# A decoder block on one Trainium2 core: residual rows parked in DRAM during the input projection, their SBUF lent to split weights

## The chip, the cores and the metric

The kernel runs on one core of a Trainium2 chip, as one program in one launch. The metric is the device time in microseconds (us) of an execution; lower is better. Three runs of the kernel before gave 1945.76, 1946.14 and 1946.44 us.

## The reference

One decoder layer over 256 rows (tokens) of 2048 features, in f32:

```python
h = h + 0.5 * swiglu(rms_norm(h, ffn1_norm), ffn1_w_gu, ffn1_w_down)     # D_FF = 5632
h = h + hybrid_mixer(rms_norm(h, mix_norm), w_in, ..., w_out)
h = h + 0.5 * swiglu(rms_norm(h, ffn2_norm), ffn2_w_gu, ffn2_w_down)
gate = sigmoid(rms_norm(h, ple_norm) @ ple_w_gate)
h = h + gate * (p @ ple_w_proj)
out = rms_norm(h, final_norm)
```

`hybrid_mixer` makes one input projection `n @ w_in` (14 blocks of 512 columns and 16 extra columns, a and b). Eight heads go through a short convolution, SiLU, normalisation and a gated delta rule in chunks of 64 rows, which needs a triangular system solved per chunk; eight heads go through stick-breaking attention. The two results, one of them gated, are concatenated and multiplied by `w_out` (4 blocks of 512 columns).

## The kernel before, in words

**Weights.** TensorE gets every f32 product as three matmuls of rounded operands: a weight W is split into `whi`, W rounded (a cast on ScalarE, ACT, line 74), and `wlo = W - whi` (a subtraction on VectorE, DVE, line 75). `weight_pair` (lines 64 to 76) handles a pair of 128-row slices, 128 x 1024 values or 512 KB: the load into a `raw` tile is issued on SP's queue (line 71), then come cast and subtraction. There are four `raw` buffers and three each of `whi` and `wlo`. `next_weights` (lines 82 to 97) hands out pairs in the order of the list `order` and emits loads and splits ahead of their use; with `LEAD = 2` the pair in use and two more are split. `accumulate` (lines 99 to 112) takes a pair and issues its 12 matmuls of 512 columns (lines 109 to 111: `whi` by the high part of the activations, `wlo` by the high part, `whi` by the low part).

**Stages.** The first feed-forward layer (`ffn`), the mixer (`mixer`, lines 746 to 1314), the second feed-forward layer, and the gated embedding with the final norm. The residual rows `h` lie in one SBUF tile of 128 x 2 x 2048 f32 (line 139). In the mixer `h` is read by the norm that precedes it (three of its four blocks by way of `transposed`, lines 162 to 186, the last on TensorE at line 212), and then not until the output projection adds to it (line 1310).

**The mixer's side work.** Each of the 14 column blocks of the input projection takes 8 pairs, 112 pairs in all. After each pair `lanes.step()` advances four lists of generators by one piece each: `conv_silu` (from line 927: transposes `tr_p` on TensorE, 12 multiply-adds on DVE at line 938, SiLU on ACT at line 944 or 947, transposes back `tr_b` at line 806), `decay_and_beta` (line 833: the 16 extra columns, whose weights `wabr` are loaded on ACT's queue at line 835, split into `wpad` at lines 852 and 853, and multiplied on TensorE at lines 848 and 849, `abT`), `system` and `chain` (the triangular solve, 31 steps of `pm` and `sol` on DVE at lines 1056 and 1058, then small matmuls), and `stick`. So TensorE's stream holds the pairs' matmuls with small matmuls of the side work between them, and these need results of DVE and ACT.

**Order.** The code is written in program order; a scheduler then fixes each engine's own order before the program is built. On the chip every engine, and every queue of transfers (SP's, ACT's, POOL's), runs its instructions in that order and waits at the first that isn't ready. `wo` are the products of the output projection; its third quarter of each block comes from `sbT` and the last from the second `dnT`, which `gate` (from line 1256) makes: multiply, transpose by way of DRAM (`scr`, then `yT`, on SP's queue), split (lines 1272 and 1273).

Of the kernel before, what the change touches and what calls it, by code (L numbers as in the profile page):

```python
# [34 lines left out]

NS_BEHIND = 2

PLAIN = {"1": 2, "2": 1}
EPS = 1e-6
QSCALE = P ** -0.5  # L40
# [3 lines left out]
def block_kernel(ctx, tc, a, out):  # L44
    nc = tc.nc
# [15 lines left out]
    dr = ctx.enter_context(tc.tile_pool(name="dr", bufs=1, space=bass.MemoryType.DRAM))  # L61


    def weight_pair(src, pool=wp, bufs=3, parts=1):

        raw = wp.tile([P, 2, NB], F32, tag="raw", name="raw", bufs=4)
        hi = pool.tile([P, 2, NB], F32R, tag="whi", name="whi", bufs=bufs)
        lo = pool.tile([P, 2, NB], F32R, tag="wlo", name="wlo", bufs=bufs)
        for i in range(parts):
            j = slice(2 * i // parts, 2 * (i + 1) // parts)  # L70
            nc.sync.dma_start(out=raw[:, j, :], in_=src[:, j, :])
        for i in range(parts):
# [9 lines left out]
    def next_weights():  # L82

        ahead = max(1, min(LEAD, done[1] // 2))
        while done[0] < len(order):
            kind, src = order[done[0]]
            if kind != "load" and sum(k == kind for k, _ in split) > (ahead if kind == "pair" else 1):
                break
            done[0] += 1
            if kind == "load":  # L90
                src()
            elif kind == "sum":
                split.append((kind, next(src.sums)))
            else:
                split.append((kind, weight_pair(src, parts=2 if not done[1] and not split else 1)))
        done[1] += 1
        return split.pop(0)[1]

# [37 lines left out]

    gains = cp.tile([P, 4, KD], F32, tag="gains", name="gains")
    nc.scalar.dma_start(out=gains, in_=a["gains"])
    h = act.tile([P, 2, D], F32, tag="h", name="h")

    ident = cp.tile([P, P], F32, tag="ident", name="ident")
    make_identity(nc, ident)
# [45 lines left out]
    def norm_block_behind(nT, which, j, tmp):  # L188

        hi, lo = nT  # L190
        yield
        tT = tmp()
        yield from transposed(lambda t: h[:, t, block(j)], tT)
        for kk in range(4):
            split_scaled(*(n[j][:, kk, :].rearrange("p (t q y) -> p (t q) y", t=2, q=4) for n in (hi, lo)),
                         tT[:, :, :, 32 * kk:32 * kk + 32].rearrange("p t q y -> p (t q) y"),
                         gains[:, which, 4 * j + kk:4 * j + kk + 1])
            if kk == 1:
                yield

    def norm_block(nT, which, j, tmp, new=mx_ps):

        if j < 3:
            lanes.add(0, norm_block_behind(nT, which, j, tmp))
            return
        hi, lo = nT
        for kk in range(2):
            tr = new("tr_n")
            for q in range(2):
                k = 4 * j + 2 * kk + q  # L210
                for t in range(2):
                    nc.tensor.transpose(tr[:, q * T + t * P:q * T + (t + 1) * P],
                                        h[:, t, k * P:(k + 1) * P], ident)
            for q in range(2):
                k = 4 * j + 2 * kk + q
                split_scaled(hi[j][:, 2 * kk + q, :], lo[j][:, 2 * kk + q, :],
                             tr[:, q * T:(q + 1) * T], gains[:, which, k:k + 1])

    def sumsq(stat, t, c, col):
        n = c.stop - c.start  # L220
        junk = act.tile([P, NB], F32, tag="junk", name="junk", bufs=1)
        nc.scalar.activation(junk[:, 0:n], h[:, t, c], AF.Square, accum_out=stat[:, t, col:col + 1])

    def block(j):
        return slice(j * NB, (j + 1) * NB)
# [185 lines left out]
        return made  # L411

    ffn_plan = {"1": plan("1")}
    order += [("pair", a["w_in"][blk][g]) for blk in W_IN_ORDER for g in range(KD // 2)]
    order += [("pair", a["w_out"][nb][g]) for nb in range(4) for g in range(KD // 2)]
    ffn_plan["2"] = plan("2")
    order += [("pair", a["w_pg"][2][g]) for g in range(KD // 2)] + [("pair", a["w_pp"][2])]
# [46 lines left out]
    def ffn(n, nT, r, scale, next_norm, stat):  # L464
        xs = picker(*nT)
        late = callable(r)
        with tc.tile_pool(name="ffn", bufs=1) as fp:
# [43 lines left out]
            for group, todo in ffn_plan[n]:  # L511
# [15 lines left out]
                for kind, one in todo:  # L527
# [19 lines left out]
                    if dn:  # L547
                        nb = group.nb + b
                        for t in range(2):
                            hb = h[:, t, block(nb)]  # L550
                            nc.vector.scalar_tensor_tensor(out=hb, in0=outs[t], scalar=scale, in1=hb,
                                                           op0=ALU.mult, op1=ALU.add)
                            if group.last:
                                sumsq(stat, t, block(nb), nb)
# [45 lines left out]
    def first_loads():  # L600

        todo = [(t, j) for t in range(2) for j in range(4)]
        xs_at = {2 * k - 1 if k < 4 else k + 3: 2 * k for k in range(1, KD // 2)}
        for i in range(1, 16):
            if i in xs_at:
                load_x(xs_at[i])
            if 5 <= i < 13:
                t, j = todo[i - 5]
                nc.sync.dma_start(out=h[:, t, block(j)], in_=a["x"][t * P:(t + 1) * P, block(j)])
            if 7 <= i < 15:  # L610
                t, j = todo[i - 7]
                sumsq(stat, t, block(j), j)
            yield
        r_first.append(rstd(stat))
# [4 lines left out]
    def r1():  # L619
# [8 lines left out]

    stat = new_stat()
    nT = mixer(tc, nc, a, act, mm_ps, mx_ps, accumulate, picker, new_nT, norm_block, sumsq, block, lanes, transposed,  # L630
               nT, r, h, stat, ident, mhalf)
    r = rstd(stat)

    stat = new_stat()
# [4 lines left out]
    with tc.tile_pool(name="fin", bufs=1) as fp:  # L639
# [18 lines left out]
        def gated(e, gt, c, t, col):  # L658

            n = c.stop - c.start  # L660
            s = act.tile([P, NB], F32, tag="nat", name="sg", bufs=4)[:, 0:n]
            nc.scalar.activation(s, gt, AF.Sigmoid, scale=r[:, t:t + 1])
            nc.vector.tensor_tensor(out=s, in0=e, in1=s, op=ALU.mult)
            nc.vector.tensor_tensor(out=h[:, t, c], in0=h[:, t, c], in1=s, op=ALU.add)
            sumsq(stat, t, c, col)
            nc.vector.tensor_tensor(out=hf[:, t, c], in0=h[:, t, c], in1=fg[:, c], op=ALU.mult)

        def embed(new):
            e = [new("e") for _ in range(2)]
# [74 lines left out]


def mixer(tc, nc, a, act, mm_ps, mx_ps, accumulate, picker, new_nT, norm_block, sumsq, block, lanes, transposed,
          nT, r, h, stat, ident, mhalf):
    xs = picker(*nT)
    C64 = P // 2
    CONV, CHAIN, STICK, SYSTEM = 0, 1, 2, 3  # L750
# [2 lines left out]
    with tc.tile_pool(name="mix", bufs=1) as mp, \  # L753
# [521 lines left out]
            dnT[1].append(tl)  # L1275


        lanes.add(CHAIN, decay_and_beta())
        for hg in range(2):
            for part in (1, 0, 2):  # L1280
# [12 lines left out]
            lanes.add(CONV, gate(y, hg))  # L1293


        nxt = new_nT()

        def pick(k):
# [6 lines left out]
        for nb in range(4):  # L1305
            d = [mm_ps("wo") for _ in range(2)]
            accumulate(d, pick, KD)
            for t in range(2):
                hb = h[:, t, nb * NB:(nb + 1) * NB]
# [68 lines left out]
```

## Time and profile before

| | |
|---|---|
| median of three runs | 1946.14 us (1945.76 to 1946.44) |
| span of the profiled execution, first to last instruction | 1944.1 us |
| median less span | 2.0 us |
| TensorE (PE) busy | 1927.9 us, 99% |
| DVE busy | 1603.2 us, 82% |
| ACT busy | 1163.4 us, 60% |
| moved by DMA | 475.06 MB, 244 GB/s on the mean |

The runs give no time for the profiled execution apart from its span; the median of the runs lies 2.0 us above the span, and these 2.0 us are taken as what lies around it. Busy time of PE is modelled from pipelined matmuls, each of which shows some 0.39 us though one starts about every 0.23 us; so what PE loses is read from the distance of starts. In a row of instructions the number in brackets is the idle time of the engine before it and what ended that. The input projection lies at about 694 to 1065 us of the span, the output projection at 1065 to 1154 us.

### The profile page before, as it was taken

The numbers are of one execution on the slowest core, as the hardware profiler recorded it, in microseconds if no ns is written. First come the engines' busy times: TensorE is split into PE (matmuls) and PEld (weight loads), VectorE is DVE, ScalarE is ACT, GpSimd is POOL, SyncE is SP. The second block draws the span as 40 slices with busy tenths as digits, with TensorE's granted clock in tenths as the row PEclk, the third lists the DMA queues.
The fourth block names the chain that finished last, engine by engine and source line by source line (L and its number), as shares of the span: only waits on it lengthen the run. The fifth ranks groups of instructions, "written<-read, shape, count | busy, mean of one in ns | idle before, by whom it ended". The sixth has DMA issues, their size and how long they took to land.

```text
span 1944.1 us, 24295 instructions
## 1 busy us (share of the span) xinstructions
PE 1927.9 (99%) x8882; PEld 1593.1 (82%) x8882; DVE 1603.2 (82%) x1743; ACT 1163.4 (60%) x1358; POOL 148.8 (8%) x226
## 2 busy tenths in 40 slices
PE   9999999999999999999999999999999999999998
PEld 7888888888888888878788888888888888888887
DVE  7879988998889866797856679899888998889965
ACT  6655656566665567654555456566565755657654
POOL 0010110000001000010100000011000100001000
PEclk9999999999999999999999999999999999999999
DMA  8778898898898765556464776788898988989864
GB/s 306 269 217 291 256 292 272 248 296 247 269 288 255 224 218 171 173 167 218 159 215 157 243 278 229 236 268 285 260 278 253 306 257 261 264 263 273 253 212 147
DMA packets 144183, 475.06 MB, mean 244 GB/s; under 512 B 19648, under 2 KB 47296, under 8 KB 129856
## 3 DMA queue, kind: packets, MB, share of 16 engines
q1 hardware_dynamic: 104896, 293.78, 43.6%
q0 software_dynamic: 25920, 160.44, 29.9%
q10 hardware_dynamic: 13248, 19.30, 3.3%
q8 instruction: 69, 1.13, 0.2%
q14 instruction: 50, 0.41, 0.1%
HBM read 451.44 MB, written 22.02 MB: 244 GB/s over the span
## 4 chain that ended last, share of the span: by engine, by line
PE 91%; DVE 6%; issue 1%; DMA 1%; ACT 1%; POOL 0%; SPq 0%; POOLq 0%; DVEq 0%; ACTq 0%
PE d L540 5%; PE d L541 5%; PE d L542 5%; PE u L541 5%; PE u L542 5%; PE u L540 5%; PE g L541 4%; PE g L542 4%; PE pj L109 4%; PE pj L110 4%; PE pj L111 4%; PE g L540 4%; PE g L335 4%; PE g L334 4%; PE g L336 4%; PE u L334 3%
## 5 line engine op out<-in xcount | busy, mean ns | idle before, releaser
L74 ACT CAST whi<-raw 128x1024 fp32r<-128x1024 f32 (+1 forms) x489 | 511.7, 1050 | 420.0 <-PE pj L111 108.9
L75 DVE TENSOR_TENSOR wlo<-raw,whi 128x1024 fp32r<-128x1024 f32 (+1 forms) x489 | 590.8, 1217 | 155.8 <-ACT whi L74 153.1
L296 DVE TENSOR_TENSOR slo<-R,shi 128x2048 fp32r<-128x2048 f32 (+2 forms) x224 | 444.4, 1987 | 99.9 <-ACT shi L295 99.7
L295 ACT CAST shi<-R 128x2048 fp32r<-128x2048 f32 (+2 forms) x224 | 374.0, 1673 | 185.6 <-DVE R L304 74.4
L109 PE MATMUL pj<-whi,nTh 128*128 128x512 f32 x448 | 179.4, 401 | 0.0
L110 PE MATMUL pj<-wlo,nTh 128*128 128x512 f32 x448 | 175.3, 391 | 1.4 <-DVE wlo L75 1.4
L111 PE MATMUL pj<-whi,nTl 128*128 128x512 f32 x448 | 174.9, 390 | 0.0
L541 PE MATMUL d<-wlo,hTh 128*128 128x512 f32 x448 | 174.4, 389 | 0.0
L542 PE MATMUL d<-whi,hTl 128*128 128x512 f32 x448 | 174.0, 389 | 0.0
L540 PE MATMUL d<-whi,hTh 128*128 128x512 f32 x448 | 173.1, 390 | 0.0
L541 PE MATMUL g<-wlo,nTh 128*128 128x512 f32 x400 | 156.1, 390 | 0.6 <-DVE wlo L75 0.6
L540 PE MATMUL g<-whi,nTh 128*128 128x512 f32 x400 | 154.9, 390 | 1.2 <-ACT whi L74 0.9
L542 PE MATMUL g<-whi,nTl 128*128 128x512 f32 x400 | 155.9, 390 | 0.0
L541 PE MATMUL u<-wlo,nTh 128*128 128x512 f32 x400 | 155.7, 389 | 0.1
L542 PE MATMUL u<-whi,nTl 128*128 128x512 f32 x400 | 155.6, 389 | 0.0
L540 PE MATMUL u<-whi,nTh 128*128 128x512 f32 x400 | 154.2, 389 | 0.0
L304 DVE TENSOR_TENSOR R<-R 128x2048 f32<-128x2048 f32 (+2 forms) x68 | 135.4, 1991 | 0.1
L110 PEld LDWEIGHTS pj<-wlo,nTh 128*128 128x128 f32 x448 | 84.2, 188 | 19.2 <-DVE wlo L75 3.0
L540 PEld LDWEIGHTS d<-whi,hTh 128*128 128x128 f32 x448 | 84.1, 188 | 17.9 <-ACT hTh L499 0.7
L542 PEld LDWEIGHTS d<-whi,hTl 128*128 128x128 f32 x448 | 84.1, 188 | 17.7
L111 PEld LDWEIGHTS pj<-whi,nTl 128*128 128x128 f32 x448 | 84.1, 188 | 17.5
L541 PEld LDWEIGHTS d<-wlo,hTh 128*128 128x128 f32 x448 | 84.1, 188 | 17.4
(327 smaller groups left out, 3482.5 us busy)
## 6 DMA issues: line engine op xcount, KB each, us to landing
raw<-in_w_gu SPq DMA_DIRECT2D x199, 512.0 KB, 5.7
raw<-in_w_down SPq DMA_DIRECT2D x112, 512.0 KB, 6.4
raw<-in_w_in SPq DMA_DIRECT2D x112, 512.0 KB, 3.4
R<-in_w_gu2q POOLq DMA_DIRECT2D x54, 1024.0 KB, 8.1
R<-in_w_gu1q POOLq DMA_DIRECT2D x48, 1024.0 KB, 8.7
raw<-in_w_out SPq DMA_DIRECT2D x32, 512.0 KB, 4.4
R<-in_w_down11q POOLq DMA_DIRECT2D x12, 768.0 KB, 6.8
R<-in_w_down12q POOLq DMA_DIRECT2D x12, 768.0 KB, 6.3
```

Source lines behind the costliest of these rows:

```text
L74: nc.scalar.copy(hi[:, j, :], raw[:, j, :])
L75: nc.vector.tensor_tensor(out=lo[:, j, :], in0=raw[:, j, :], in1=hi[:, j, :], op=ALU.subtract)
L109: nc.tensor.matmul(outs[t], xh[:, c], whi[:, j, :], start=st, stop=False)
L110: nc.tensor.matmul(outs[t], xh[:, c], wlo[:, j, :], start=False, stop=False)
L111: nc.tensor.matmul(outs[t], xl[:, c], whi[:, j, :], start=False, stop=sp)
L295: keep(nc.scalar.copy(hi, w))
L296: nc.vector.tensor_tensor(out=lo, in0=w, in1=hi, op=ALU.subtract)
L304: keep(nc.vector.tensor_tensor(out=self.raw[x], in0=self.raw[x], in1=self.raw[y], op=ALU.add))
L334: nc.tensor.matmul(out, xh, whi[:, g, :], start=st, stop=False, skip_group_check=True)
L540: nc.tensor.matmul(out, xh[:, c], whi[:, j, :], start=st, stop=False, skip_group_check=True)
L541: nc.tensor.matmul(out, xh[:, c], wlo[:, j, :], start=False, stop=False, skip_group_check=True)
L542: nc.tensor.matmul(out, xl[:, c], whi[:, j, :], start=False, stop=sp, skip_group_check=True)
```

## The change

`h` becomes four tiles of 128 x 2 x 512 (one per column block), four buffers of one tag. After the norm is taken, each block is written to a DRAM tile `saved`; when the input projection has been issued, four new tiles of the tag are made and read back. In between, the tag's four buffers hold `whi` and `wlo` of two "spare" pairs. The table `SPARE` says which of the 112 pairs are spare: those with index i from 12 on where i mod 5 is 2, and from 24 on where i mod 5 is 4, so that from there on three of five pairs rotate through the three old buffers and two of five through the spare ones: the pair in use and four more are split. Nothing else of the arithmetic changes.

```diff
+SPARE = {2: 10, 4: 22}
...
-    def weight_pair(src, pool=wp, bufs=3, parts=1):
+    def weight_pair(src, pool=wp, bufs=3, parts=1, tags=("whi", "wlo")):
         raw = wp.tile([P, 2, NB], F32, tag="raw", name="raw", bufs=4)
-        hi = pool.tile([P, 2, NB], F32R, tag="whi", name="whi", bufs=bufs)
-        lo = pool.tile([P, 2, NB], F32R, tag="wlo", name="wlo", bufs=bufs)
+        hi = pool.tile([P, 2, NB], F32R, tag=tags[0], name="whi", bufs=bufs)
+        lo = pool.tile([P, 2, NB], F32R, tag=tags[1], name="wlo", bufs=bufs)
...
-                split.append((kind, weight_pair(src, parts=2 if not done[1] and not split else 1)))
+                pool, tags, bufs = (act, ("h", "h"), 4) if kind == "spare" else (wp, ("whi", "wlo"), 3)
+                split.append((kind, weight_pair(src, pool, bufs, 2 if not done[1] and not split else 1, tags)))
...
-    h = act.tile([P, 2, D], F32, tag="h", name="h")
+    def new_h():
+        h[:] = [act.tile([P, 2, NB], F32, tag="h", name="h", bufs=4) for _ in range(4)]
...
-    order += [("pair", a["w_in"][blk][g]) for blk in W_IN_ORDER for g in range(KD // 2)]
+    for i, (blk, g) in enumerate((blk, g) for blk in W_IN_ORDER for g in range(KD // 2)):
+        order.append(("spare" if i % 5 in SPARE and i >= SPARE[i % 5] else "pair", a["w_in"][blk][g]))
...
+        saved = dp.tile([P, 4, 2, NB], F32, tag="saved", name="saved")
+
+        def save():
+            for j in range(4):
+                yield
+                nc.sync.dma_start(out=saved[:, j], in_=h[j])
+
+        lanes.add(STICK, save())
         lanes.add(CHAIN, decay_and_beta())
...
+        new_h()
+        for j in range(4):
+            nc.sync.dma_start(out=h[j], in_=saved[:, j])
         nxt = new_nT()
```

The diff moves instructions on several engines. In the rows below line numbers of the changed kernel are some higher than before (110 is 113 there, 848 is 861, 852 is 865, 853 is 866, 877 is 890, 938 is 951, 169 is 181, 1070 is 1083).

On PE, in the seventh pair of the input projection, where the extra columns' first matmuls `abT` stand among the pairs' `pj`; before:

```order
L109 MATMUL pj<-whi,nTh 128x512 x2
L110 MATMUL pj<-wlo,nTh 128x512
L848 MATMUL abT<-nTh,wpad 128x256
L849 MATMUL abT<-nTl,wpad 128x256
L848 MATMUL abT<-nTh,wpad 128x256
```

and now:

```order
L112 MATMUL pj<-whi,nTh 128x512 x2
L113 MATMUL pj<-wlo,nTh 128x512
L114 MATMUL pj<-whi,nTl 128x512
L113 MATMUL pj<-wlo,nTh 128x512
L861 MATMUL abT<-nTh,wpad 128x256
```

The first `abT` has moved ahead by ten matmuls of 512 columns: these stand before it in the order before and behind the eight `abT` now. The same place on ACT, which issues the load `wabr` and makes `wpad` from it; before:

```order
L158 ACTIVATE nTh<-tT,gains 128x256 x4
L74 CAST whi<-raw 128x1024
L765 DMA conv<-in_conv 128x96
L767 DMA onorm<-in_dn_out_norm 128x128
L769 DMA alog<-in_a_log 128x8
L771 DMA dtb<-in_dt_bias 128x8
L835 DMA wabr<-in_w_ab 128x256
L74 CAST whi<-raw 128x1024 x2
L852 CAST wpad<-wabr 128x4x16 x2
```

and now:

```order
L170 ACTIVATE nTh<-tT,gains 128x256 x4
L778 DMA conv<-in_conv 128x96
L780 DMA onorm<-in_dn_out_norm 128x128
L782 DMA alog<-in_a_log 128x8
L784 DMA dtb<-in_dt_bias 128x8
L848 DMA wabr<-in_w_ab 128x256
L76 CAST whi<-raw 128x1024
L890 ACT_TABLE_LOAD
L890 ACTIVATE ea<-alog 128x8
L865 CAST wpad<-wabr 128x4x16
L76 CAST whi<-raw 128x1024
```

One cast now stands behind the five loads instead of ahead of them, and a table load with `ea` stands between that cast and the first `wpad`.

On DVE, in the sixth convolution of the mixer (`cT` are its multiply-adds, `X<-Z` and `tb<-nat` are transposes of other side work), about 867 to 877 us of the span; before:

```order
L938 SCALAR_TENSOR_TENSOR cT<-tr_p,conv,cT 128x253 x2
L75 TENSOR_TENSOR wlo<-raw,whi 128x1024
L938 SCALAR_TENSOR_TENSOR cT<-tr_p,conv,cT 128x255 x2
L938 SCALAR_TENSOR_TENSOR cT<-tr_p,conv,cT 128x254 x2
L938 SCALAR_TENSOR_TENSOR cT<-tr_p,conv,cT 128x253
L75 TENSOR_TENSOR wlo<-raw,whi 128x1024
L938 SCALAR_TENSOR_TENSOR cT<-tr_p,conv,cT 128x253
L169 STREAM_TRANSPOSE tb<-nat 128x512 x2
L75 TENSOR_TENSOR wlo<-raw,whi 128x1024
L1070 STREAM_TRANSPOSE X<-Z 32x8x32
```

and now:

```order
L951 SCALAR_TENSOR_TENSOR cT<-tr_p,conv,cT 128x253 x2
L1083 STREAM_TRANSPOSE X<-Z 32x8x32
L77 TENSOR_TENSOR wlo<-raw,whi 128x1024
L951 SCALAR_TENSOR_TENSOR cT<-tr_p,conv,cT 128x255 x2
L951 SCALAR_TENSOR_TENSOR cT<-tr_p,conv,cT 128x254
L77 TENSOR_TENSOR wlo<-raw,whi 128x1024
L951 SCALAR_TENSOR_TENSOR cT<-tr_p,conv,cT 128x253
L951 SCALAR_TENSOR_TENSOR cT<-tr_p,conv,cT 128x254
L181 STREAM_TRANSPOSE tb<-nat 128x512
L951 SCALAR_TENSOR_TENSOR cT<-tr_p,conv,cT 128x253
L181 STREAM_TRANSPOSE tb<-nat 128x512
```

One `X<-Z` and one `tb` have moved ahead of the convolution's last multiply-add. From `kdec` (line 971 before), some 80 instructions earlier, to that last multiply-add the two kernels have otherwise the same instructions on DVE, 14 `wlo` among them; each `wlo` belongs to the pair two further on.

On SP, the restores among the loads of the output projection's weights, new:

```order
L73 DMA raw<-in_w_out 128x1024 x2
L1319 DMA h<-saved 128x1024 x2
L73 DMA raw<-in_w_out 128x1024 x2
L1319 DMA h<-saved 128x1024 x2
L73 DMA raw<-in_w_out 128x1024
L185 DMA scr<-tb 128x512
```

The first two restores wait for the matmuls of pair 107, the last two for those of pair 109, and the loads of the fourth and the sixth output pair stand behind them. The four saves stand on SP too: one ahead of the `scr` of the first block's norm in the last product of the first feed-forward layer, the others between the loads of the sixth to the eighth pair of the input projection.

## Rows read from the trace of the kernel before

**Rows 1.** The page, part 1: busy us, share of the span, instructions.

```profile
PE 1927.9 (99%) x8882; PEld 1593.1 (82%) x8882; DVE 1603.2 (82%) x1743; ACT 1163.4 (60%) x1358; POOL 148.8 (8%) x226
```

**Rows 2.** Busy us by engine in a stretch, clock, DMA share, GB/s.

```profile
830.00:878.00 48.00, 46.60 (x227) 37.83 (x226) 47.00 (x87) 30.37 (x53) 4.23 (x3) 1.00 0.57 178
```

**Rows 3.** Timeline of PE: start, us, engine, line, operation, count, idle before.

```profile
841.84 0.39 PE L109 MATMUL pj<-whi,nTh 128*128 128x512 f32 x1
842.84 0.50 PE L110 MATMUL pj<-wlo,nTh 128*128 128x512 f32 x1 [0.61 <-DVE wlo L75]
...
845.49 0.39 PE L109 MATMUL pj<-whi,nTh 128*128 128x512 f32 x1
846.33 0.50 PE L110 MATMUL pj<-wlo,nTh 128*128 128x512 f32 x1 [0.46 <-DVE wlo L75]
...
859.17 0.39 PE L109 MATMUL pj<-whi,nTh 128*128 128x512 f32 x1
859.88 0.50 PE L110 MATMUL pj<-wlo,nTh 128*128 128x512 f32 x1 [0.33 <-DVE wlo L75]
```

**Rows 4.** Timeline of PE, waits for the side work.

```profile
926.91 0.79 PE L1109 MATMUL vp<-R,Z 128*128 128x128 f32 x5 [1.15 <-DVE R L1130]
...
944.65 0.68 PE L1221 MATMUL at<-ident,st 128*128 128x128 f32 x3 [0.66 <-DVE st L1214]
```

**Rows 5.** Timeline of DVE: its first and its next idle time around the stretch.

```profile
830.02 0.69 DVE L971 TENSOR_TENSOR kdec<-tr_b,ss 128x512 f32<-128x512 f32 x1 [1.93 <-POOL ss L925]
...
883.46 0.42 DVE L1020 TENSOR_TENSOR AT<-kk,dec 128x256 f32<-128x256 f32 x1 [1.84 <-PE kk L1019]
```

**Rows 6.** Timeline of DVE at the end of the sixth convolution.

```profile
873.20 0.47 DVE L938 SCALAR_TENSOR_TENSOR cT<-tr_p,conv,cT 128x253 f32<-128x253 f32 x1
873.59 1.29 DVE L169 STREAM_TRANSPOSE tb<-nat 128x512 f32<-128x512 f32 x2
...
875.92 0.42 DVE L1070 STREAM_TRANSPOSE X<-Z 32x256 f32<-32x256 f32 x1
```

**Rows 7.** Timeline of ACT at the same place.

```profile
873.75 1.28 ACT L947 ACT_TABLE_LOAD   x1 [0.34 <-DVE cT L938]
875.05 1.06 ACT L947 ACTIVATE cT<-cT 128x1024 f32<-128x1024 f32 x1
```

**Rows 8.** Timeline of PE at the same place.

```profile
877.03 1.03 PE L806 MATMUL tr_b<-ident,cT 128*128 128x128 f32 x8
```

**Rows 9.** Timeline of ACT (ACTq is its queue of transfers) at the extra columns.

```profile
703.10 1.05 ACT L74 CAST whi<-raw 128x1024 fp32r<-128x1024 f32 x1
706.30 0.45 ACTq L835 DMA_DIRECT2D wabr<-in_w_ab  x1
...
710.47 0.39 ACT L852 CAST wpad<-wabr 128x64 fp32r<-128x64 f32 x2 [0.93 <-DMA wabr<-in_w_ab]
```

**Rows 10.** Timeline of DVE at the same place.

```profile
710.75 0.38 DVE L853 TENSOR_TENSOR wpad<-wabr,wpad 128x64 fp32r<-128x64 f32 x2 [1.59 <-ACT wpad L852]
```

**Rows 11.** Timeline of PE at the same place.

```profile
711.69 0.28 PE L848 MATMUL abT<-nTh,wpad 128*128 128x256 f32 x1
```

**Rows 12.** Timeline of SP's queue of transfers.

```profile
694.98 18.90 SPq L71 DMA_DIRECT2D raw<-in_w_in  x8
...
1069.35 0.33 SPq L173 DMA_DIRECT2D scr<-tb  x1
...
1073.40 3.20 SPq L183 DMA_DIRECT2D yT<-scr  x4
```

**Rows 13.** Busy us, clock, DMA share, GB/s: the busiest stretch seen.

```profile
1150.00:1172.00 22.00, 21.80 (x100) 17.64 (x100) 18.79 (x29) 12.65 (x18) 0.80 (x1) 1.00 0.85 338
```

**Rows 14.** DMA issues: out<-in, engine, count, KB each, median us to landing.

```profile
raw<-in_w_in SPq DMA_DIRECT2D x112, 512.0 KB, 3.4
```

**Rows 15.** Timeline of ACT at the split of the second `dnT`.

```profile
1080.27 1.14 ACT L1272 CAST dnT<-yT 128x512 fp32r<-128x512 f32 x2
```

**Rows 16.** Timeline of PE, first use of the second `dnT`.

```profile
1081.83 0.39 PE L109 MATMUL wo<-whi,dnT 128*128 128x512 f32 x1
```

More of the change, by code (lines that the diff above doesn't have):

```diff
@@ L138, in block_kernel, with h_at @@
     nc.scalar.dma_start(out=gains, in_=a["gains"])
-    h = act.tile([P, 2, D], F32, tag="h", name="h")
+    h = []
+    def new_h():
+        h[:] = [act.tile([P, 2, NB], F32, tag="h", name="h", bufs=4) for _ in range(4)]
+    def h_at(t, c):
+        j = c.start // NB
+        return h[j][:, t, c.start - j * NB:c.stop - j * NB]
+    new_h()
     ident = cp.tile([P, P], F32, tag="ident", name="ident")
@@ L192, in norm_block_behind @@
         tT = tmp()
-        yield from transposed(lambda t: h[:, t, block(j)], tT)
+        yield from transposed(lambda t: h[j][:, t, :], tT)
         for kk in range(4):
@@ L212, in norm_block @@
                     nc.tensor.transpose(tr[:, q * T + t * P:q * T + (t + 1) * P],
-                                        h[:, t, k * P:(k + 1) * P], ident)
+                                        h_at(t, slice(k * P, (k + 1) * P)), ident)
             for q in range(2):
@@ L221, in sumsq @@
         junk = act.tile([P, NB], F32, tag="junk", name="junk", bufs=1)
-        nc.scalar.activation(junk[:, 0:n], h[:, t, c], AF.Square, accum_out=stat[:, t, col:col + 1])
+        nc.scalar.activation(junk[:, 0:n], h_at(t, c), AF.Square, accum_out=stat[:, t, col:col + 1])
     def block(j):
@@ L549, in ffn @@
                         for t in range(2):
-                            hb = h[:, t, block(nb)]
+                            hb = h[nb][:, t, :]
                             nc.vector.scalar_tensor_tensor(out=hb, in0=outs[t], scalar=scale, in1=hb,
@@ L608, in first_loads @@
                 t, j = todo[i - 5]
-                nc.sync.dma_start(out=h[:, t, block(j)], in_=a["x"][t * P:(t + 1) * P, block(j)])
+                nc.sync.dma_start(out=h[j][:, t, :], in_=a["x"][t * P:(t + 1) * P, block(j)])
             if 7 <= i < 15:
@@ L630, in block_kernel @@
     nT = mixer(tc, nc, a, act, mm_ps, mx_ps, accumulate, picker, new_nT, norm_block, sumsq, block, lanes, transposed,
-               nT, r, h, stat, ident, mhalf)
+               nT, r, h, stat, ident, mhalf, new_h)
     r = rstd(stat)
@@ L663, in gated @@
             nc.vector.tensor_tensor(out=s, in0=e, in1=s, op=ALU.mult)
-            nc.vector.tensor_tensor(out=h[:, t, c], in0=h[:, t, c], in1=s, op=ALU.add)
+            nc.vector.tensor_tensor(out=h_at(t, c), in0=h_at(t, c), in1=s, op=ALU.add)
             sumsq(stat, t, c, col)
-            nc.vector.tensor_tensor(out=hf[:, t, c], in0=h[:, t, c], in1=fg[:, c], op=ALU.mult)
+            nc.vector.tensor_tensor(out=hf[:, t, c], in0=h_at(t, c), in1=fg[:, c], op=ALU.mult)
         def embed(new):
@@ L746, in mixer @@
 def mixer(tc, nc, a, act, mm_ps, mx_ps, accumulate, picker, new_nT, norm_block, sumsq, block, lanes, transposed,
-          nT, r, h, stat, ident, mhalf):
+          nT, r, h, stat, ident, mhalf, new_h):
     xs = picker(*nT)
@@ L1293, in mixer @@
             lanes.add(CONV, gate(y, hg))
+        new_h()
+        for j in range(4):
+            nc.sync.dma_start(out=h[j], in_=saved[:, j])
         nxt = new_nT()
@@ L1308, in mixer @@
             for t in range(2):
-                hb = h[:, t, nb * NB:(nb + 1) * NB]
+                hb = h[nb][:, t, :]
                 nc.vector.tensor_tensor(out=hb, in0=d[t], in1=hb, op=ALU.add)
```

## The prediction, as made before the run

> **What bounds the kernel now.** I read the page's first part, then the mixer by its own stretches, since the change touches only the mixer and the places where `h` is handed over. PE is busy for 1927.9 of 1944.1 us [rows 1]: the reader should take from it that no other engine's mean matters, only moments at which PE stands still. Twelve matmuls a pair, one each 0.227 us (an estimate from the distance of starts; the rows show 0.23), make 2.72 us a pair. The timeline of PE shows where it stands still on account of split weights: three times in 20 us, before the first `wlo` matmul of a pair, released by DVE's subtraction [rows 3]. By starts, 842.84 - 841.84 is 1.00, 0.77 more than a step; 846.33 - 845.49 leaves 0.61; 859.88 - 859.17 leaves 0.48. The sum is 1.9 us, and I found no others in the input projection. Two larger single waits there, 1.15 and 0.66 us idle, are for side work, `R` and `st` [rows 4], not for weights. So what a deeper lead of splits can give back at all is 1.9 us, and all waits of both kinds come to 3.7. A measurement of this kernel tells about 0.2%, 3.9 us, from no change.
>
> Why is `wlo` late there? DVE works without a marked gap from `kdec` at 830.02, which waited for POOL, to 883.46 [rows 5], and is busy 47.00 of 48 us [rows 2]. In this stretch DVE itself is the limit, not the number of buffers: more buffers let weights be split earlier, but the same DVE instructions must pass, and other results of DVE that PE needs lie among them.
>
> **The change part by part.**
>
> *The 1.9 us of `wlo` waits.* By the order, each `wlo` from `kdec` on stands where it stood, but for the pair two further on: two pairs are 5.4 us of cover, against the largest wait of 0.77. These waits go: -1.9.
>
> *What is late next.* PE's next need of DVE in that stretch is `tr_b` of the sixth convolution. Before, the last `cT` ends at 873.20 + 0.47 = 873.67 [rows 6], ACT loads a table from 873.75 for 1.28 and applies SiLU until 875.05 + 1.06 = 876.11 [rows 7]; PE takes it at 877.03 without waiting [rows 8]. That leaves 0.92 us of slack, and PE had been held up by 1.9 before. DVE's time at this place is fixed by its work since 830.02, not by PE, so a PE that comes 1.9 us earlier only waits here. The order also puts one `X<-Z` (0.42) and one `tb` (half of 1.29, 0.65) ahead of the last `cT` [rows 6]: 1.07 us later, and up to 0.5 more (an estimate) if the transfer that writes `Z` isn't there yet. The table load and SiLU follow later by as much. Against PE's old time this is 1.07 - 0.92 = +0.15 to 1.57 - 0.92 = +0.65. So the stretch nets +0.4 in place of -1.9; bounds -1.9 (all waits saved and the gate moved away) and +1.2 (both moved pieces wait).
>
> The Trainium skill has a rule that speaks for more: in "Perfetto Trace Analysis", section "Identifying Performance Opportunities", the same gap, repeating on the engine that should be saturated, can mean too few buffers. The trace agrees with it as to the gap [rows 3] and against it as to the cause, DVE's 47.00 of 48 us. By that rule the term would be -1.9, which is a rival below.
>
> *Start.* The first `abT` moves ahead of ten matmuls: it was taken at 711.69 [rows 11], now PE comes to it at 711.69 - 2.27 = 709.4. Its weights: the issue of `wabr` at 706.30 and the cast of `wpad` at 710.47, 0.93 of it waiting for the landing [rows 9], so 4.17 from issue to cast; then DVE's low part from 710.75 [rows 10]. On ACT one cast of 1.05 [rows 9] moved behind the issue, so that goes out at some 705.2 and lands at 709.3; cast and DVE part (0.19 each; the two casts take 0.39) put the first `wpad` at about 709.85. PE waits 0.45. To this comes traffic: three saves of 0.52 MB are issued with the loads from 694.98 on [rows 12]. Four loads and three saves make 3.67 MB, at 338 GB/s, the most I saw in a stretch [rows 13], 10.9 us; from 695 to 705.1 are 10.1. A backlog of 0.8 in front of `wabr` would add as much; I take half of it, 0.35: +0.8 together. Bounds 0 (transfers land sooner with a shorter queue) and 2.5 (all 10.9 us of traffic and `ea` ahead of the cast count).
>
> What speaks against the change here is that `wabr` goes out on ACT's queue and the saves on SP's. The Trainium skill, "DMA: Bandwidth & Descriptors", section "Issuing engines are not separate DMA queues", says that transfers of all issuing engines share the same 16 DMA engines and interleave; no row here shows a load of ACT's queue held up by SP's. By that rule the 0.8 of backlog would count in full and the term be +1.25.
>
> *Saves otherwise.* 512 KB each; a load of this size lands 3.4 us after its issue [rows 14]. The first goes out before the last product of the first feed-forward layer, the others by about 705. The first spare pair is the thirteenth; its split runs no earlier than some 20 us into the projection (715). Cover: some 6 us; 0. If it were gone, the first spare cast would wait, with two pairs split ahead: still 0 up to 5 us.
>
> *Second burst, 906 to 945.* The same nine `wlo` stand between the chain's pieces; `onat` (0.6) moves ahead of the second `R`, one reduction (0.3) away from `st`. So `R` comes some 0.3 later, `st` some 0.3 earlier [rows 4]: 0, bounds -0.4 and +0.5.
>
> *Restores.* They are the added wait. On SP the first two wait for the matmuls of pair 107, four pairs (10.9 us) before the output projection at 1065, about 1054; the last two for those of pair 109, about 1060. Behind them are loads of the fourth and sixth output pair, `scr` at 1069.35 and `yT` at 1073.40 [rows 12]. The loads are issued some 8 us before their need and land in 3.4 [rows 14], so they have cover. `scr` and `yT` have little: `dnT` is cast until 1080.27 + 1.14 = 1081.41 [rows 15] and used at 1081.83 [rows 16], 0.42 of slack; any more passes to PE one for one. From 1054.7 to 1067.6 (the first `scr`) loads want 0.52 MB per 2.72 us, 2.5 MB, and restores 2.1: 4.6 MB at 338 GB/s [rows 13] are 13.6 us, 0.7 more than the 12.9 there are. 0.7 - 0.4 = +0.3; bounds 0 and 2. PE adds to `h` first at about 1087, far behind.
>
> *Nothing else.* The second feed-forward layer has the same order on every engine; splits in the middle of the mixer have 3 us of slack and lose nothing.
>
> Sum: +0.4 + 0.8 + 0 + 0.3 = **+1.5**. Against the profiled span, 1944.1 + 1.5 = 1945.6; the median stands 2.0 above the span, so **1947.6 us**.
>
> **The rivals.**
>
> *A, the buffers pay.* The `wlo` waits go (-1.9), the moved `cT` falls where PE isn't held, start and end are hidden: 1946.14 - 1.9 = 1944.2. For it: the three waits [rows 3] are by name those that the lead removes. Against: the full DVE [rows 2] and 0.92 of slack at `tr_b` [rows 7, 8]. If the two waits for `R` and `st` went too, -3.7, it would be 1942.4; a faster result beyond 3.9 us needs more yet, some of the short idle times that rows 1 sum up (16 us in all).
>
> *B, slower: the restores in front of the gate's transpose.* All restores need 2.1 MB / 338 GB/s = 6.2 us. If they are still under way when `scr` and `yT` are issued, `dnT` is late by what is left. Half of it, 3.1 above the sum without the end term: +1.2 + 3.1 = +4.3, 1950.4; all: +7.4, 1953.5. It decides (beyond 3.9 us) from a delay of about 2.7 us. For it: 0.42 of slack, and an output stage that already moves much. Against: the restores are issued 7 to 13 us ahead of `scr`.
>
> *C, the lead doesn't come.* `raw` keeps four buffers and DVE has no time free, so that splits never run four pairs ahead by 840: the three waits stay (0), start and end are paid (+0.8 + 0.3): 1947.2. Against: the load of a pair waits for the split four before it, as now, and DVE has idle time before 830.
>
> **How the numbers follow.** The forecast 0.52, A 0.22, B 0.14, C 0.12. The forecast's own range by its bounds is 1945 to 1950. Faster by over 0.2% (below 1942.2) is only A's far end: 0.05. Slower (above 1950.0) is B and 0.02 of the forecast's upper end: 0.16. Within 0.2%: 0.79. The range 1944.0 to 1951.0 takes in the forecast, C, most of A and the mild half of B; outside are A's far end and the bad half of B, under 0.2.
>
> **What would show it.** Right: no `wlo` wait of PE in 840 to 862; a wait of PE for `cT` at `tr_b` near 877 of 1.5 to 2.5 us; one for `wpad` at about 709.5; `dnT` used within a microsecond of the old distance from the start of the output projection. Wrong: `tr_b` taken without a wait (then A), `dnT` cast over 2 us later against the output projection (B), `wlo` named as a releaser in 840 to 862 (C), or any new wait of PE in the second feed-forward layer.

## The result and the profile after

The changed kernel takes 1950.03 us (median of 16 runs, 1948.22 to 1951.50) against 1946.53 of the kernel before in the same comparison (16 runs): a ratio of 1.0018, 95% interval 1.001 to 1.0025. That is 3.5 us slower, beyond the scatter of this comparison though still under the 0.2% named in the prediction. The profiled execution has a span of 1947.9 us against 1944.1. Engines are as busy as before [rows 1]; the first part of the page:

```profile
PE 1929.5 (99%) x8882; PEld 1594.7 (82%) x8882; DVE 1603.4 (82%) x1743; ACT 1162.9 (60%) x1358; POOL 147.0 (8%) x226
```

The waits of PE, longest first (engine, tile and line <- what it waited for: us in total, times, longest). The `wlo` waits of the input projection [rows 3] have left the list; a wait at `tr_b`, which was none before [rows 8], leads it, and `vp` and `at` [rows 4] wait 0.35 and 0.48 longer than before:

```profile
PE tr_b L819 <- ACT cT L960: 2.1, 1, 2.1
PE vp L1122 <- DVE R L1143: 1.5, 1, 1.5
PE at L1234 <- DVE st L1227: 1.1, 1, 1.1
```

PE runs the same matmuls in both kernels, so the clearest view is how far the same matmul has moved. This table is worked out from the starts of the 512-column matmuls in the timelines of PE: the median of the later kernel's start less that of before, and set to 0 at 700 us. (Before 700 us two executions of one kernel differ by up to 1.3 us, at the very start of the program; at 700 us the change's profile runs 0.32 us ahead of that of before, so times of the two as they stand differ by 0.32 less than the table says.) "again" is a second profiled execution of the changed kernel, "base" one of the kernel before; the other names are experiments below.

```
us of the kernel before   720    870    887    933    960   1062   1160
passed since the left    abT    wlo   tr_b     vp     at   start   end
base                     0.00  -0.02  -0.03   0.02  -0.02  -0.02  -0.03
the change               0.75  -1.26   2.70   3.06   3.53   3.53   3.51
again                    0.91  -1.13   1.38   1.76   2.25   2.25   2.26
fill                     1.12  -0.87   1.48   1.70   2.16   2.16   2.16
order                    1.00  -1.08   0.30  -0.66   1.64   1.69   1.70
no_spare                 1.25   1.22   1.22   1.23   1.22   1.22   1.06
late_save                0.00  -2.06   0.80   1.18   1.65   1.65   1.66
late_fill                0.00  -2.06   0.67   0.83   1.27   1.27   1.27
fill_all                 1.38  -0.64   1.97   3.18   3.90   3.90   3.87
tab_late                 0.97  -0.99  -0.41  -0.45  -0.07  -0.05   1.65
tab2                     1.43  -0.57   0.14   0.57   0.82   0.82   0.80
best                     0.00  -2.07  -1.30  -1.34  -1.11  -1.12  -1.11
best_again               0.00  -2.02  -1.32  -1.39  -1.18  -1.18  -1.21
```

The base line shows that, for the kernel before, two executions agree to some 0.05 us here. The start is less steady: the change, again, fill, order, no_spare and fill_all have the same order there and lose 0.75 to 1.38. The change's line reads, from left to right: +0.75 at the start, -2.01 at the `wlo` waits, +3.96 at `tr_b`, +0.36 at `vp`, +0.47 at `at`, nothing at the end: 3.5 us. So the buffers do bring what they can bring, and one matmul group takes twice that back.

The place itself. The timeline of PE in the change (start, us; in brackets the idle time before and what ended it):

```profile
875.22 0.39 PE L114 MATMUL pj<-whi,nTl 128*128 128x512 f32 x1
877.71 1.45 PE L819 MATMUL tr_b<-ident,cT 128*128 128x128 f32 x8 [2.09 <-ACT cT L960]
878.95 3.26 PE L1032 MATMUL kk<-knq 128*128 128x256 f32 x8
881.86 0.58 PE L112 MATMUL pj<-whi,nTh 128*128 128x512 f32 x1
```

From the start of `tr_b` to the next `pj` are 4.15 us. Before, they were 2.41, from 877.03 [rows 8] to this row:

```profile
879.44 0.59 PE L109 MATMUL pj<-whi,nTh 128*128 128x512 f32 x1
```

The wait is one thing, and what comes behind it another: by stretch of the change (us; busy time of PE, PEld, DVE, ACT, POOL; then granted clock, DMA share, GB/s) the clock is

```profile
877.70:879.00 1.30, 1.29 (x9) 1.30 (x10) 0.56 (x2) 1.30 (x2) 0.00 (x0) 0.73 0.69 178
879.00:881.80 2.80, 2.80 (x8) 2.26 (x8) 2.77 (x5) 1.50 (x3) 0.00 (x0) 0.52 0.51 175
```

0.52 is about the lower of TensorE's two levels, 1.2 of 2.4 GHz. Ahead of it the engine had started nothing for 2.49 us (875.22 to 877.71). Why is `tr_b` late? The timelines of DVE and of ACT in the change:

```profile
856.04 1.00 DVE L1069 TENSOR_TENSOR pm<-sol,L 128x216 f32<-128x216 f32 x1
...
873.39 0.85 DVE L951 SCALAR_TENSOR_TENSOR cT<-tr_p,conv,cT 128x253 f32<-128x253 f32 x2
874.17 0.69 DVE L181 STREAM_TRANSPOSE tb<-nat 128x512 f32<-128x512 f32 x1
874.80 0.43 DVE L951 SCALAR_TENSOR_TENSOR cT<-tr_p,conv,cT 128x253 f32<-128x253 f32 x1
```

```profile
875.30 1.28 ACT L960 ACT_TABLE_LOAD   x1 [2.22 <-DVE cT L951]
876.60 1.06 ACT L960 ACTIVATE cT<-cT 128x1024 f32<-128x1024 f32 x1
```

The last `cT` ends at 875.23 (874.80 + 0.43) instead of 873.67 [rows 6], with one `tb` right ahead of it; table load and SiLU follow to 877.66 (876.60 + 1.06) instead of 876.11 [rows 7].

### The profile page after: what moved, and what is told of

Its sections match the earlier page's. It is cut to its first block, busy times and chain, and to the rows that moved or that the text cites. A ratio compares the mean times of both kernels' runs of the same rounds, so it can differ in the third digit from the quotient of the medians.

```text
span 1947.9 us, 24311 instructions
## 1 busy us (share of the span) xinstructions
PE 1929.5 (99%) x8882; PEld 1594.7 (82%) x8882; DVE 1603.4 (82%) x1743; ACT 1162.9 (60%) x1358; POOL 147.0 (8%) x226
## 4 chain that ended last, share of the span: by engine, by line
PE 88%; DVE 7%; DMA 2%; issue 2%; ACT 1%; POOL 0%; ACTq 0%; SPq 0%; DVEq 0%; POOLq 0%
PE d L553 5%; PE d L554 5%; PE d L555 5%; PE u L554 5%; PE u L555 5%; PE u L553 5%; PE g L554 4%; PE g L555 4%; PE g L553 4%; PE pj L112 4%; PE pj L114 4%; PE pj L113 4%; PE g L347 4%; PE g L346 4%; PE g L348 4%; PE u L346 3%
```

## The experiments

Theory 1: the buffers save 2.0 us; the late `cT` makes PE wait at `tr_b`, and the idle engine then loses its clock. Theory 2: `tr_b` and `kk` are slow for another reason. Theory 3: the traffic of saves and restores costs most. Each comparison has its own runs of the kernel before, with medians from 1946.21 to 1946.54; "against before" is against those.

**fill.** Ahead of `tr_b` of the sixth convolution:

```diff
+            f = mx_ps("fil")
+            for _ in range(20):
+                nc.tensor.transpose(f[:, 0:P], ident, ident)
```

> The change, with 20 transposes of the identity (128x128, about 0.11 us each, 2.2 us in all, result not used) put on TensorE just ahead of tr_b of the sixth convolution, where it stands idle for 2.1 us. Theory 1 (the idle time itself costs: the granted clock falls to 0.52 behind it, and tr_b and kk take 4.15 us in place of 2.41): tr_b still starts near 877.7, but the granted clock stays at 1.00 and the next pj starts about 1.7 us earlier than in the change, 880.1 in place of 881.86; total about 1.7 us below the change. Theory 2 (the slow tr_b and kk come from late operands or traffic): tr_b to the next pj stays at 4.1 us and the time stays that of the change.

PE in the profile:

```profile
874.71 2.35 PE L943 MATMUL fil<-ident 128*128 128x128 f32 x20
877.01 1.09 PE L819 MATMUL tr_b<-ident,cT 128*128 128x128 f32 x8
877.94 1.89 PE L1039 MATMUL kk<-knq 128*128 128x256 f32 x8
879.48 0.58 PE L112 MATMUL pj<-whi,nTh 128*128 128x512 f32 x1
```

As theory 1 has it for this execution: the full clock, 2.47 us from `tr_b` to `pj`. But the median is 1949.37 (10 runs, 1946.48 to 1952.06; ratio 1.0013, 1.0004 to 1.0022), only 0.7 below the change and not 1.7 (3.0 above before in its own comparison, where the change stands 3.5 above): as a statement on the median the expectation missed.

**order.** The three `X<-Z` one step later and pinned, the first `tb` pinned:

```diff
-            for _ in range(5):
+            for _ in range(6 if hg == 0 else 5):
...
+                    tc.keep_in_program_order(tx)
...
+                tc.keep_in_program_order(tb)
```

> The change, with the X and tb transposes pinned behind the last multiply-add of the sixth convolution on VectorE (1.07 us of work off its front). Theory 1: the last cT ends near 874.2, SiLU near 876.6, tr_b waits about 1.1 us instead of 2.1, and after a wait that short the granted clock stays at 1.00 (in both kernels it does after waits of 1.1 to 1.5 us): next pj near 879.0, 2.8 us earlier than in the change; the later stages may shift by some tenths. Theory 2 (the moved pieces do not matter, ACT or something else makes tr_b late): tr_b stays near 877.7.

```profile
876.84 1.09 PE L821 MATMUL tr_b<-ident,cT 128*128 128x128 f32 x8 [1.17 <-ACT cT L962]
877.77 1.89 PE L1034 MATMUL kk<-knq 128*128 128x256 f32 x8
879.31 0.58 PE L112 MATMUL pj<-whi,nTh 128*128 128x512 f32 x1
```

As theory 1 expected: the wait falls to 1.17, the clock stays, and `tr_b` costs 1.4 instead of 4.0 (table, 870 to 887; 2.5 in again below, where the clock stayed too). Later stages give some back: the three `X<-Z` (1.36 together) now stand right ahead of `st` on DVE, and `at` waits 2.1. Median 1948.17 (ratio 1.0012, 1.0002 to 1.0022). The runs fall into two groups, six from 1947.3 to 1948.4 and four from 1949.3 to 1950.8. Of theory 2 this rules out that `tr_b` is late for another reason: moving two pieces of DVE's work moves it.

**no_spare.** `SPARE = {}`, restores pinned at their place on SP.

> The change without spare pairs: saves, restores and four h tiles stay, all 112 pairs rotate through the three old buffers. Theory 1: the start costs the same as in the change (abT ten matmuls earlier, +0.75 against before), the three wlo waits are back (1.9 us) and there is no wait at tr_b; after the start everything stands +0.75 behind the kernel before: 1946.5 + 0.75 = 1947.3. Theory 3 (traffic of saves and restores is what costs most of the 3.5 us): 1949 or more.

1947.13 (ratio 1.0004, 0.9994 to 1.0013), 0.8 above before. In the table all of its 1.2 us lies at the start, and 0 from 720 to 1062 us; the `wlo` waits are back (1.6 us, 4 times). So the handing over of `h` costs about a microsecond at the start and nothing at the end, and the rest of the 3.5 comes only when spare pairs are there. Theory 3 is out.

**late_save.** The saves some four pairs later and pinned.

> The change with the four saves pinned some four pairs later on the sync engine's queue, so that the order of ScalarE and TensorE at the start is that of before. Theory 1: the start costs nothing (shift at 715 us about -0.3 instead of +0.4), tr_b still waits 2 us and loses the clock: 0.75 below the change, 1949.3. Theory 3 (saves' traffic costs wherever it stands): the shift at 715 to 725 us stays at +0.4 or more.

```profile
876.95 1.09 PE L819 MATMUL tr_b<-ident,cT 128*128 128x128 f32 x8 [2.64 <-ACT cT L960]
877.88 1.89 PE L1032 MATMUL kk<-knq 128*128 128x256 f32 x8
879.42 0.58 PE L112 MATMUL pj<-whi,nTh 128*128 128x512 f32 x1
```

The start is free, as expected (0.00 at 720). The wait at `tr_b` is the longest of all, and yet the clock did not fall here: a miss of "loses the clock" for this execution. The median is 1948.98, near the 1949.3 expected, with three runs at 1946.6 to 1947.4 and seven at 1948.8 to 1950.3. That looks like a loss that strikes in some executions.

**again.** The changed kernel unaltered.

> The changed kernel once more, on the same chip as the next two, for a second profiled execution and more executions. Theory 1 (after the wait at tr_b the clock falls in most executions, not in all): 3 to 3.5 us above before, in two groups some 1.7 us apart, and a profile that shows either 4.1 us from tr_b to the next pj with a granted clock near 0.5 to 0.7, or 2.4 us and 1.00. Theory 4 (the clock falls there always and what varies is something else): one group, and 4.1 us again.

```profile
877.11 1.09 PE L819 MATMUL tr_b<-ident,cT 128*128 128x128 f32 x8 [2.30 <-ACT cT L960]
878.04 1.89 PE L1032 MATMUL kk<-knq 128*128 128x256 f32 x8
879.58 0.58 PE L112 MATMUL pj<-whi,nTh 128*128 128x512 f32 x1
```

```profile
877.70:879.00 1.30, 1.30 (x10) 1.20 (x9) 0.97 (x1) 1.30 (x3) 0.00 (x0) 1.00 0.89 317
879.00:881.80 2.80, 2.80 (x14) 2.35 (x13) 2.73 (x7) 0.91 (x2) 0.00 (x0) 1.00 0.61 151
```

Theory 1's second case: the same kernel, a wait as long, a clock of 1.00 and 2.47 us from `tr_b` to `pj`. DMA moved more in the first stretch than in the change (317 against 178 GB/s), so traffic there isn't what slowed `tr_b` and `kk`; with the clock of 0.73 and 0.52 this rules out theory 2. This execution took 1947.43, the profiled one of the change 1949.60; the median is 1949.99 (11 runs, two at 1947.4 and 1948.2, nine from 1949.4 to 1952.4, so no clean pair of groups). Theory 4 (it always falls there) is out.

**fill_all.** As fill, with 13 more transposes ahead of `vp` and 10 ahead of the first `at`.

> The change with transposes of the identity on TensorE ahead of its three longest waits: 20 at tr_b, 13 at vp, 10 at the first at. Theory 1: the engine is nowhere idle for over 1 us in the mixer, so the clock stays at 1.00 in nearly all executions: the start (+0.75), the wlo waits (-2.0), tr_b (+2.2 of plain waiting), vp and at (+0.8) remain, together 1.8 above before, 1948.2, with few executions over 1949.5. Theory 4 (the transposes do not keep the clock, or it falls for another reason): the same time as the change.

1949.41 (ratio 1.0014, 1.0005 to 1.0023), a miss by 1.2. In the profile the start took 1.38 where 0.75 was expected, `tr_b` 2.6 where 2.2 was, and what follows to 960 us 1.9 where 0.8 was. The transposes themselves hardly hold up PE: the shift grows by 0.1 at `vp` (927.84 is the end of `R`, 927.99 the start of `vp`) and by 1.1 at `op` behind it, which waits 0.79 for `vn`, because on DVE a `wlo` and a `pm` now stand ahead of `vn` that in fill stand behind it; and by 0.7 at `at`, where PE still waits 0.28 for `st` behind the transposes. Ten of eleven runs lie at 1950.2 or below, and the median doesn't stand above what its own profile adds up to (1946.51 + 3.87 = 1950.4), whereas for the change it does (1946.51 + 2.26 = 1948.8 by the execution with the full clock, 1949.99 measured).

**late_fill.** late_save with the 20 transposes of fill.

> The change with late saves, as in run late_save, and with 20 transposes of the identity on TensorE ahead of tr_b, as in run fill. Theory 1: start 0, wlo -2.0, plain waiting at tr_b +2.5, vp and at +0.8, and no clock loss there: 1.3 above before, with few executions of a second group; late_save had two groups, 1946.6 to 1947.4 and 1948.8 to 1950.3. Theory 4 (transposes do not keep the clock): the two groups of late_save again, median near 1949.

1948.79 (ratio 1.0011, 1.0002 to 1.0019) where 1947.5 was expected; late_save had 1948.98. A second miss of the filler on the median, with the full clock again in its profile.

**tab_late**, **tab2.** Late saves, and behind the last ACT copy of the sixth convolution a SiLU of one element, so that the table is loaded before DVE is done (the diff is that of tab2, which writes it to the scratch tile `junk`; tab_late writes it to a new tile of four bytes a row). In both the scheduler also puts the first `tb` back behind the last `cT`, so they mend two things at `tr_b`, 1.28 us of table load and 0.65 of `tb`:

```diff
+                    if (part, hg, c) == (2, 1, 3):
+                        junk = act.tile([P, NB], F32, tag="junk", name="junk", bufs=1)
+                        tc.keep_in_program_order(nc.scalar.activation(junk[:, 0:1], one, AF.Silu))
```

> The change with two repairs: the saves four pairs later (start as before), and a one-element SiLU on ScalarE behind the last copy of the sixth convolution, so that the table load of 1.28 us runs before the last multiply-add and not behind it; by the order this also puts one tb back behind the last cT. Theory 1: SiLU ends near 875.7 by the clock of before, tr_b waits about 0.7 us in place of 2.1 to 2.6, no clock loss: 2.0 saved at the wlo waits, 0.7 lost at tr_b, start 0; vp and at as in the change (+0.8): 1946.4 - 0.5 = 1945.9, faster than the change by 4. Theory 5 (VectorE is the limit again right behind, the gain is taken back at vp and at): waits there grow by what tr_b gives, and it ends at 1946.4 to 1947.5.

> The kernel of run tab_late with the one-element SiLU written into an existing scratch tile instead of a new tile of four bytes a row. In tab_late's profile the output projection ran with steps of 0.233 us in place of 0.227 (1.5 us in all) and the second abT wait of 0.7 us had no releaser. If the new small tile did that (it shifts the tiles behind it), both go: 1945.5 to 1946, faster than before by 0.5 to 1. If it is scatter of that execution, the median stays near 1948.4.

tab_late 1948.39 (ratio 1.0006, 0.9997 to 1.0015), tab2 1946.54 (1.0001, 0.9992 to 1.0010). In both, `tr_b` gives only 0.6 to 0.7 back (table, 870 to 887), as theory 1 expected, and theory 5 is out as far as that goes. The slow output projection of tab_late (+1.7 from 1062 to 1160) isn't in tab2. The medians, 1.88 and 0.33 above before, differ by about as much, so it isn't that one execution's alone; whether the four-byte tile was its cause isn't shown, since one profile of each is all there is. Both lost 1.0 to 1.4 at the start. tab2's timelines of ACT and of PE show why:

```profile
706.32 0.80 ACTq L848 DMA_DIRECT2D wabr<-in_w_ab  x1
...
712.42 0.39 ACT L865 CAST wpad<-wabr 128x64 fp32r<-128x64 f32 x2 [2.90 <-DMA wabr<-in_w_ab]
```

```profile
713.02 0.36 PE L861 MATMUL abT<-nTh,wpad 128*128 128x256 f32 x1 [1.20 <-issue]
```

`wabr` took 6.1 us from issue to cast, against 4.2 before [rows 9] and 4.05 in late_save (705.46 to 709.51). Of the four profiles with saves at this place two have about 4 us (late_save, late_fill) and two about 6 (tab_late, tab2): its landing varies from execution to execution. That the saves beside it are the reason isn't shown.

**base.** The kernel before, unaltered.

> The kernel before once more, for a second profiled execution: how far two executions of one kernel differ at each stage. If the +0.2 to +0.6 us at about 1170 and at about 1920 belong to the change, they are not seen here; if they are scatter of executions, they are. Time 1946.5.

1945.91. Against the first one its profile gains 0.2 at about 1170 us and another 0.5 at about 1920: what looked like a cost of the change there is scatter.

**best**, **best_again.** tab2 with the saves nine pairs later than in the change (five later than in tab2) and `SPARE = {2: 30, 4: 32}`.

> The change with three repairs: the one-element SiLU (into the scratch tile), the saves nine pairs later, and the first spare pairs at index 32 and 34 instead of 12 and 24, so that the saves have time and nothing of them runs beside the load of wabr. Theory 1: start 0 (no wait for abT), wlo -2.0, tr_b +0.7 (a wait of about 0.5 us, granted clock 1.00), vp and at +0.7 at most: 0.6 below before or a little more, 1945.5. Theory 5 (what is won at wlo is lost again at the later waits on VectorE, whatever the start): 1946.2 or more. A difference of 0.6 us is too small for the comparison of times; the distance of starts between the two profiles at 700, 865, 885 and 960 us tells it.

> The kernel of run best once more, for more executions: 1944.82 against 1946.27 there, an interval that reaches just past 1. If the gain of about 1.1 us between 800 and 950 us in its profile belongs to the kernel, the median is again 1 to 1.5 us below before; if it was scatter of that set of executions, the two are equal.

1944.82 (11 runs, 1944.19 to 1946.15) against 1946.27; then 1945.36 against 1946.54. Ratios 0.9993 (0.9984 to 1.0002) and 0.9995 (0.9986 to 1.0004): each interval just reaches 1, but the medians lie 1.45 and 1.18 below before, and both profiles place 1.1 to 1.2 us between 840 and 960. PE and ACT of best at the place:

```profile
874.75 1.09 PE L819 MATMUL tr_b<-ident,cT 128*128 128x128 f32 x8 [0.56 <-ACT cT L963]
```

```profile
868.64 1.28 ACT L955 ACT_TABLE_LOAD   x1
869.94 0.20 ACT L955 ACTIVATE junk<-one 128x1 f32<-128x1 f32 x1
...
873.64 1.06 ACT L963 ACTIVATE cT<-cT 128x1024 f32<-128x1024 f32 x1 [0.46 <-DVE cT L951]
```

The table load is done long before the last `cT`, and the SiLU starts as soon as that is there. By its profiles this version is ahead of the kernel before by what the buffers save (2.0) less what is left at `tr_b` (0.7) and behind it (0.2); the medians agree, though neither comparison of times alone tells it from no change.

## Why the prediction was right, and where its size was off

The sign, the range and the class held: 1950.03 lies within 1944.0 to 1951.0, slower by less than 0.2%. The size didn't: +1.5 was forecast and +3.5 came, at the upper edge of the forecast's own range (1945 to 1950). By the table the parts are: start 0.75 for 0.8, the stretch 1.95 for 0.4, the second burst 0.83 for 0, the end 0 for 0.3.

*The `wlo` waits, -1.9.* Right: -2.01, in every kernel with spare pairs and in none without. The rule of the Trainium skill ("Perfetto Trace Analysis", "Identifying Performance Opportunities", same gaps can mean too few buffers) holds for the gaps: with more buffers they go. The time didn't follow, because the saturated DVE had another result to deliver in the same stretch. order tells its share from that of the moved pieces: with both put back, `tr_b` still takes 1.38 of the 2.08 saved; the two pieces cost the other 1.1 (2.51 in again).

*The stretch, +0.4.* This is the step that failed, and by its price. The mechanism was named: the last `cT` 1.07 to 1.57 later (1.56 measured by the times of the profiles: some 1.1 for the moved `X<-Z` and `tb`, the rest DVE's own earlier delay, 0.15 of it at `kdec` already and most of what is left by a `pm` that took 1.00, 0.58 before), SiLU late, PE waiting 1.5 to 2.5 (2.09 measured). As plain waiting it is +0.5 (again: -2.04 and +2.51). The prediction set a wait at its own length, "against PE's old time", and left out what a wait of that length can do to PE behind it. In the profiled execution the granted clock was 0.73 and then 0.52, and `tr_b` to `pj` took 4.15 instead of 2.47: 1.7 more, +1.95 for the stretch. Of the four waits of over 2 us in the profiles (`tr_b` in the change, in again and in late_save, `at` in order) it happened behind one, and behind none of the waits of 1.6 us or less.

How often it strikes isn't shown, since the clock by stretch is seen only in profiles. The medians speak for often: the change, late_save, fill and late_fill stand 0.9 to 1.3 above what their own profiles with the full clock (for the change that of again) add up to, while order, no_spare, tab_late, tab2, best and fill_all stand between 1.0 below and 0.2 above. The fillers didn't take that microsecond out of fill and late_fill.

One record bears on the executions that weren't profiled: each run's mean granted clock, to three digits (0.998 for the profiled execution of the change, 0.999 for that of again). In the change, again, fill and order the 32 runs at 0.998 or below are on the mean 1.1 to 2.1 us slower than the 15 at 0.999 of the same kernel (again: 1950.47 against 1948.75); in the kernel before, in the five later comparisons, the difference is -0.1 to 0.4. All four slower runs of order are at 0.998 or below. So it looks as if the clock falls in many executions of these four kernels, in fill in spite of the transposes. It isn't proof: the profiled executions of late_fill and tab2 have 0.998 too, and 1.00 at the place. In late_save (1.2, with three runs at 0.998) and late_fill (0.3) the sign is weaker, and another cause may take their microsecond: their profiles show no loss at the start, but those of tab_late and tab2, with the same late saves, lose 0.97 and 1.43 there. Which it is stays open.

*The start, +0.8.* 0.75 and 0.91 came, but the agreement is luck. The prediction had 0.45 for `wpad` and 0.35 for half of a backlog. ACT and PE in the change:

```profile
705.79 0.44 ACTq L848 DMA_DIRECT2D wabr<-in_w_ab  x1
706.33 1.05 ACT L76 CAST whi<-raw 128x1024 fp32r<-128x1024 f32 x1 [3.66 <-DMA saved<-h]
...
709.19 0.25 ACT L865 CAST wpad<-wabr 128x64 fp32r<-128x64 f32 x1 [0.26 <-DMA wabr<-in_w_ab]
```

```profile
707.97 0.61 PE L112 MATMUL pj<-whi,nTh 128*128 128x512 f32 x2
708.70 0.50 PE L113 MATMUL pj<-wlo,nTh 128*128 128x512 f32 x1
709.04 0.40 PE L114 MATMUL pj<-whi,nTl 128*128 128x512 f32 x1
709.28 0.40 PE L113 MATMUL pj<-wlo,nTh 128*128 128x512 f32 x1
709.79 0.36 PE L861 MATMUL abT<-nTh,wpad 128*128 128x256 f32 x1
```

`abT` starts at 709.79, foretold for 709.85, by two errors that cancel: `wabr` was issued at 705.79 and not at 705.2, and it took 3.40 from issue to cast and not 4.17, so no backlog shows. (By the table's measure `abT` and the issue each come 0.3 later still.) It costs 0.28 there (709.28 to 709.79, less a step). Another 0.28 is the moved cast itself: it runs only when the five issues on ACT are through, so its `wlo` is late for 708.70. The remaining 0.2 lies in the steps right behind these two matmuls (0.34 from 708.70 to 709.04, where a step takes 0.23, and 0.20 between the first two `abT`, 0.12 before). I had priced the cast for what it gives `wabr` and forgotten who waits for it. On the Trainium skill's rule ("DMA: Bandwidth & Descriptors", "Issuing engines are not separate DMA queues"): tab2's 6.1 us for a load on ACT's queue beside saves on SP's would agree with it, late_save's 4.05 beside the same saves shows no delay. In the change's own profile the load wasn't held up.

*Second burst, 0.* It was +0.83. `R` is late by the `onat` between its two halves, as foretold at +0.3 (+0.36):

```profile
927.62 0.68 DVE L1142 TENSOR_TENSOR R<-ks,eG 128x512 f32<-128x512 f32 x1
928.22 0.68 DVE L1146 TENSOR_TENSOR onat<-qs,eG 128x512 f32<-128x512 f32 x1
928.82 0.68 DVE L1143 TENSOR_TENSOR R<-v,R 128x512 f32<-128x512 f32 x1
```

`st` was to come 0.3 earlier and came 0.47 later. What makes it late stays open. DVE waits there for POOL's power of `coef`, which took 2.48 us in the change (939.72), again and late_save and 1.64 before (937.59): DVE sat idle 1.53 for it, 0.31 before. But in fill and late_fill the same instruction took 1.64, and `at` moved by 0.46 and 0.44 all the same. As to its two lengths the rows show this much: in the change it starts 0.24 into a `wlo` of DVE, before it starts 0.14 ahead of one, and in fill DVE is idle beside it; whether that makes the difference wasn't tried.

*The end, +0.3.* 0.0: with 3.21 us taken off (the table's 3.53 less the 0.32 by which the change's profile runs ahead), the `scr` of 1069.35, the cast of `dnT` and its first use stand where they stood [rows 12, 15, 16], and the restores were issued at 1054.4 and 1061.9, foretold for about 1054 and 1060. SP, ACT and PE of the change:

```profile
1072.56 0.32 SPq L185 DMA_DIRECT2D scr<-tb  x1
...
1077.63 2.77 SPq L195 DMA_DIRECT2D yT<-scr  x4
```

```profile
1083.48 1.14 ACT L1285 CAST dnT<-yT 128x512 fp32r<-128x512 f32 x2
```

```profile
1085.04 0.39 PE L112 MATMUL wo<-whi,dnT 128*128 128x512 f32 x1
```

`yT` was issued 1.0 later than the shift explains and still landed in time, so the 0.42 of slack was not all there was. Rival B didn't come, nor C. Of rival A's gain of 1.9, best shows the larger part, 1.2 to 1.5 in the medians, once `tr_b` and the start are mended.

## What to carry to other kernels

Before adding buffers for a wait, see whether its producer is saturated in that stretch, and price the next result that the same producer owes. Price a wait of a busy TensorE with what the clock may take behind it, not only with its length; here, in one profiled execution, 1.7 us more behind a wait of 2.1. Where a dependent activation needs another table, load the table during the producer's work with a one-element activation ahead of it; here, with one `tb` moved back as well, the wait went from 2.1 to 2.6 us down to 0.4 to 0.6.

## What was not expected of the hardware

The granted clock fell behind an idle time of 2.09 us in one execution, and stayed at 1.00 behind 2.30 us in another of the same kernel, behind 2.64 us in late_save and behind 2.1 us in order. A load of 128 KB on ACT's queue took 4.05 or 6.1 us from issue to cast beside the same saves.
